# A one-core hybrid attention block in float32 pairs: SBUF tiles moved to other byte offsets, same instructions in the same order

## The chip, the core and the metric

The kernel runs on one core of one Trainium2 chip. The metric is the device time of one execution in microseconds; smaller is better. TensorE (PE) multiplies matrices: a load of weights (PEld) puts a block of 128 columns, the stationary operand, into the array, and a matmul then streams the moving operand past it and adds into PSUM. VectorE (DVE), ScalarE (ACT) and GpSimd (POOL) work on rows of 128 partitions. SyncE (SP) issues nearly all DMA transfers. The on-chip memory (SBUF) is 128 partitions wide; a tile has one byte offset that holds in all partitions, and this document is about these offsets.

## The reference, cut to what matters

The input x is 512 tokens by 2048 channels, float32. One decoder layer is computed:

```python
h = rmsnorm(x, norm_g)
proj = h @ w_in                     # 2048 -> 13 slices: qa, kca, vca, ksa, vsa, kwa, vwa, za, ga, qb, kb, vb, zb
# group A: 8 heads of 128, 2 kv heads; compressed, selected and windowed attention on rope'd q, k
kc = silu(blocks(rope(kca)) @ w1) @ w2 ; vc likewise     # blocks of 32 tokens, stride 16, 31 of them
o_a = g0 * attn(qa, kc, vc) + g1 * attn(qa, ksa, vsa; selected) + g2 * attn(qa, kwa, vwa; window)
y_a = o_a * silu(za)
# group B: 16 heads of 64, 2 kv heads, window of 128 tokens and a sink per head
y_b = attn(qb, kb, vb; window 128, sinks) * silu(zb)
x = x + concat(y_a, y_b) @ w_out
return rmsnorm(x, final_g)
```

With 512 tokens there are 8 blocks to select from and all are selected, so the selected attention is causal attention.

## The kernel before

**Numbers in pairs.** Nearly every float32 matrix is held as a pair: a rounded part (`F32R`, names with h or hi) and the rest (l or lo). One product of matrices is then three matmuls, written in `mm3` (lines 112 to 115): high by high, high by low, low by high. The first argument is the stationary operand, the other the moving one. The profile writes a matmul as `out<-moving,stationary`.

**Stages, in order of time.** (1) To about 55 us: `load_x` and `split_x` bring in x by its 16 slices of 128 channels, make the pair `xh`, `xl` and its sum of squares, and project the first slice of weights. (2) To 97 us: the second slice of `w0`, and the blocks tiles `F` (`blocks_part`) for the compressed keys and values. (3) To about 176 us: `tok_chunk` projects values with x as the stationary operand (moving operands of 256 and then 408 columns), interleaved with `compress_unit`, which multiplies `F` by streamed weights. (4) To about 440 us: eight heads of group A. `pair(h)` computes a head's q and gate by seven half-size products instead of eight (a Strassen-like scheme; `prod`, 128 by 256), with operand forms held in `xf`: the forms p and u lie in the `pu` tiles of the pool `yp`, the others in `xh`/`xl` and in spare halves of `KH`, `KL`, `VH`, `VL`. `attn_a` computes scores (`sp`, line 539), softmax on DVE and ACT, transposes (`tp<-ident,...`), and the products with the values (`op`). (5) To about 655 us: group B, eight pairs of heads, `proj` (128 by 512) and `softmax_b`, `attn_b`. (6) The rest: the output projection, first quarter 512 wide, the other three quarters with seven half-size products (`product`, 128 by 256), then the final norm.

Weights stream in through the pool `wp`: a raw tile (`raw`), from which ACT copies the rounded part `whi` and DVE subtracts to get `wlo` (`load_unit`, `unit`, `split_to`).

**What sets the order.** The order of instructions on each engine comes from the tile framework's planner together with `tc.issue_after`, by which the code ties a piece of work behind another.

**Where tiles lie.** A pool takes a stretch of SBUF from the left end upwards or, with `side="right"`, from the right end downwards, in the order in which pools are opened; inside it each tile is rounded up to 32 bytes. Left, from byte 1152: `const` (`ident` 512 bytes, `tab` 3588, `rstd` 16, `rstdb` 2048, `gates` 384, `gt` 64, `eps` 4), then `wp` and, before this change, `yp`, then the working pools (`s0`, later `wk`, later `so` and `wr`). Because `tab`, `rstd` and `eps` are not multiples of 64 bytes, `wp` begins at byte 7840, which is 61 times 128 and 32 more. All tiles above it have sizes that are multiples of 128 (but for a few small statistics), so **everything on the left that TensorE reads begins at 32 mod 128**: `whi`, `wlo`, the `F` and `pu` tiles, `qh`, `ql`, `ph`, `pl`. Only `ident` lies at 0. On the right the stack begins at byte 229344, which is 96 mod 128, so **`xh`, `xl`, `KH`, `KL`, `VH`, `VL`, and later `yh`, `yl` and the forms of the output projection begin at 96 mod 128**. Slices taken from these tiles start at multiples of 128 bytes from their beginning, except in the 408-column products, whose second half starts 1632 bytes in.

The built program holds 4808 matmuls with `F32R` operands: 2984 with a moving operand of 256 columns, 1536 of 512, 192 of 408 and 96 of 288. In 512 of them (464 left-with-left, which are the `pu` and `F` products, and 48 right-with-right) both operands begin at the same place mod 128; in 4200 they are 64 bytes apart; in the second halves of the 408-column products (96) they are 32 apart. The remaining matmuls are transposes and a few plain float32 ones.

Of the kernel before, what the change touches and what calls it, by code (L numbers as in the profile page):

```python
# [10 lines left out]
F32 = mybir.dt.float32  # L11
# [6 lines left out]
P = 128  # L18
S = 512
D = 2048  # L20
KT = D // P
NQ = S // P
# [5 lines left out]
CMP = 32  # L28
WARM = 40
FIRST = 1  # L30
TAB_W = 512 + NQ * CMP + 256 + 1


@with_exitstack
def hybrid_block(ctx, tc, xT, xtm, w0, w1s, w2s, wz, wq, wkb, wo0, wos, cw1, cw2, cpos, rope, tabs, sinks, gT, fg, out):
# [3 lines left out]
    def sb(name, bufs=1, side=None):  # L39
        return tc.tile_pool(name=name, bufs=bufs, side=side)  # L40

    const = ctx.enter_context(sb("const"))
    wp = ctx.enter_context(sb("wp", bufs=3))
    ident = const.tile([P, P], F32, name="ident")
    make_identity(nc, ident)
    tab = const.tile([P, TAB_W], F32, name="tab")
    dmask = tab[:, 0:512]
    cmask = tab[:, 512:512 + NQ * CMP]
    bmask = tab[:, 512 + NQ * CMP:768 + NQ * CMP]
    rowvalid = tab[:, TAB_W - 1:TAB_W]  # L50
    rstd = const.tile([P, NQ], F32, name="rstd")
    rstdb = const.tile([P, S], F32, name="rstdb")
    gates = const.tile([P, NQ, 24], F32, name="gates")
    gt = const.tile([P, KT], F32, name="gt")

    def dram(name, *shape):
        return tc.dram_tile(list(shape), F32, name=name)
# [5 lines left out]
    fd = dram("fd", 4, 2, P, KT // 4, 256)  # L63
    fw = dram("fw", 2, 2, P, KT // 4, 256)
    yd = [dram(f"yd{h}", P, S) for h in range(8)]
    eps = const.tile([P, 1], F32, name="eps")
    dve.memset(eps, EPS)
    act.activation(rstd[:, 0:1], eps, AF.Copy)

# [11 lines left out]
    def load_unit(src, width, rawp=None, opening=False):  # L81
# [9 lines left out]
                                       op=ALU.subtract).ins  # L91
        return hi, lo

    xstack = ctx.enter_context(ExitStack())
    xpool = xstack.enter_context(sb("xpool", side="right"))
    xh = xpool.tile([P, KT, S], F32R, name="xh")
# [23 lines left out]
        last["rope"] = dve.tensor_tensor(out=t2[64:128], in0=ps[0:64], in1=sin[0:64], op=ALU.mult).ins  # L120
        return t1, t2

    yp = ctx.enter_context(sb("yp"))
    p0 = ExitStack()
    s0 = p0.enter_context(sb("s0"))
    s0b = p0.enter_context(sb("s0b", bufs=2))
# [1120 lines left out]
def _tables():  # L1247
    def rope(d):
        inv = np.float32(10000.0) ** (-np.arange(0, d, 2, dtype=np.float32) / np.float32(d))
        ang = np.arange(S, dtype=np.float32)[None, :] * inv.astype(np.float32)[:, None]  # L1250
        return np.cos(ang.astype(np.float64)).astype(np.float32), np.sin(ang.astype(np.float64)).astype(np.float32)

    ca, sa = rope(128)
    cb, sb_ = rope(64)
    cb, sb_ = np.concatenate([cb, cb]), np.concatenate([sb_, sb_])
    ro = np.stack([np.concatenate([ca, ca]), np.concatenate([sa, -sa]),
                   np.concatenate([cb, cb]), np.concatenate([sb_, -sb_])], axis=1).astype(np.float32)
    p = np.arange(P)[:, None]
    j = np.arange(P)[None, :]
    caus = np.where(j <= p, 0.0, NEG)  # L1260
    band = np.where(j > p, 0.0, NEG)
    c = np.arange(CMP)[None, :]
    cm = [np.where((16 * c + 31 <= q * P + p) & (c < 31), 0.0, NEG) for q in range(NQ)]
    tabs = np.concatenate([np.zeros((P, 384)), caus] + cm + [band, caus, (p >= 31) * 1.0], axis=1).astype(np.float32)
    return np.ascontiguousarray(ro), np.ascontiguousarray(tabs)


# [51 lines left out]
```

## Time and profile before

| | |
|---|---|
| median of 3 runs | 831.02 us (827.9 to 832.21) |
| the profiled execution | 829.19 us; its span, first to last instruction, 827.4 us |
| granted TensorE clock in it | 0.997 |
| PE busy | 811.5 us, 98% of the span, 5278 matmul records |
| PE weight loads busy | 735.6 us (89%) |
| DVE / ACT / POOL busy | 662.1 (80%) / 485.6 (59%) / 89.3 us (11%) |
| DMA | 128.30 MB, 155 GB/s on average |

Matmuls are pipelined: the next starts before the last has ended, so the "mean ns of one" in the profile's groups is longer than the distance from one start to the next. The distance between starts, called the pace below, is what a product costs when TensorE is never idle. It is read from the timeline, whose first column is the start in us from the start of the span and whose second is the duration. A plain float32 matmul leaves two records.

### The profile page before, as it was taken

What the parts mean: (1) busy time and instruction counts of PE and PEld (TensorE: products, weight loads), DVE (VectorE), ACT (ScalarE), POOL (GpSimd) and SP (SyncE); (2) the same over time, 40 slices, a digit from 0 to 9 for tenths busy, and PEclk for the clock granted to TensorE, in tenths of its full rate; (3) what the DMA queues carried; (4) which work ended last, traced back from release to release, by engine and by line L of the source; (5) the groups of instructions that cost most, each with busy time, mean ns of one, the idle gap of its engine ahead of it and who ended that gap; (6) DMA issues with size and microseconds to landing.
All of it is one profiled execution on the core that took longest, in us unless ns stands there. A gap on an engine that the chain in (4) does not pass through costs nothing.

```text
span 827.4 us, 14161 instructions
## 1 busy us (share of the span) xinstructions
PE 811.5 (98%) x5278; PEld 735.6 (89%) x5278; DVE 662.1 (80%) x1311; ACT 485.6 (59%) x1026; POOL 89.3 (11%) x69
## 2 busy tenths in 40 slices
PE   9999999999999999999999999999999999999996
PEld 7788898999999999999888888888888788999996
DVE  6869786966799898999766688877677798877895
ACT  6734456564676786787665365645444647554555
POOL 3600002011001001101011121011011000110000
PEclk9999999999999999999999999999999999999998
DMA  9665885898330222522733321222222226797845
GB/s 324 194 206 166 281 290 200 265 371 284 103 111 22 99 77 92 166 90 89 251 107 102 99 92 56 74 80 74 77 76 77 77 62 241 235 251 198 244 96 203
DMA packets 52117, 128.30 MB, mean 155 GB/s; under 512 B 4945, under 2 KB 17233, under 8 KB 52049
## 3 DMA queue, kind: packets, MB, share of 16 engines
q1 hardware_dynamic: 50032, 120.59, 43.3%
q0 software_dynamic: 1728, 6.29, 4.3%
q8 instruction: 41, 0.67, 0.3%
q10 hardware_dynamic: 288, 0.52, 0.2%
q14 instruction: 28, 0.22, 0.1%
HBM read 110.31 MB, written 17.07 MB: 154 GB/s over the span
## 4 chain that ended last, share of the span: by engine, by line
PE 84%; DVE 6%; DMA 5%; issue 2%; ACT 2%; SPq 0%; DVEq 0%; ACTq 0%; POOLq 0%
PE pj L115 16%; PE pj L113 15%; PE pj L114 15%; PE bank L115 4%; PE bank L113 4%; PE oa L114 4%; PE oa L113 4%; PE oa L115 3%; PE sp L539 3%; PE bank L114 3%; PE tp L855 2%; DMA rw<-wos 1%; PE tp L577 1%; DMA xr<-xT 1%; DMA raw<-cw 1%
## 5 line engine op out<-in xcount | busy, mean ns | idle before, releaser
L115 PE MATMUL pj<-xh,wlo 128*128 128x512 f32 (+1 forms) x560 | 196.0, 350 | 2.0 <-DVE wlo L617 1.5
L113 PE MATMUL pj<-xh,whi 128*128 128x512 f32 (+1 forms) x560 | 196.2, 350 | 0.8 <-DVE t L665 0.8
L114 PE MATMUL pj<-xl,whi 128*128 128x512 f32 (+1 forms) x560 | 195.4, 349 | 0.0
L90 DVE TENSOR_TENSOR wlo<-raw,whi 128x1024 fp32r<-128x1024 f32 (+2 forms) x102 | 115.3, 1135 | 37.5 <-ACT whi L89 36.6
L89 ACT ACTIVATE whi<-raw 128x1024 fp32r<-128x1024 f32 (+1 forms) x101 | 95.2, 944 | 80.6 <-PE pj L114 24.0
L115 PEld LDWEIGHTS pj<-xh,wlo 128*128 128x128 f32 x560 | 105.3, 188 | 16.3 <-DVE wlo L617 2.2
L113 PEld LDWEIGHTS pj<-xh,whi 128*128 128x128 f32 x560 | 105.4, 188 | 14.2 <-DVE t L665 1.2
L114 PEld LDWEIGHTS pj<-xl,whi 128*128 128x128 f32 x560 | 105.3, 188 | 13.4 <-issue 0.7
L617 DVE TENSOR_TENSOR wlo<-raw,whi 128x1024 fp32r<-128x1024 f32 x49 | 61.6, 1260 | 10.3 <-ACT whi L616 9.9
L616 ACT ACTIVATE whi<-raw 128x1024 fp32r<-128x1024 f32 x49 | 51.7, 1056 | 24.7 <-PE pj L114 12.7
L113 PE MATMUL oa<-whi,yh 128*128 128x256 f32 (+1 forms) x168 | 50.1, 299 | 0.6 <-ACT yh L909 0.6
L114 PE MATMUL oa<-wlo,yh 128*128 128x256 f32 (+1 forms) x168 | 50.4, 300 | 0.2 <-DVE wlo L1147 0.2
L115 PE MATMUL oa<-whi,yl 128*128 128x256 f32 (+1 forms) x168 | 49.7, 299 | 0.0
L834 ACT ACTIVATE ttb<-ttb,mnb 128x256 f32<-128x256 f32 (+1 forms) x64 | 30.1, 471 | 26.0 <-DVE mnb L827 25.5
L509 DVE TENSOR_TENSOR pl<-tp,ph 128x512 fp32r<-128x512 f32 x56 | 37.6, 683 | 6.6 <-ACT ph L508 6.6
L508 ACT ACTIVATE ph<-tp 128x512 fp32r<-128x512 f32 x56 | 32.3, 592 | 17.9 <-PE tp L577 11.2
L114 PE MATMUL bank<-wlo,xh 128*128 128x256 f32 (+1 forms) x128 | 40.2, 316 | 0.0
L115 PE MATMUL bank<-whi,xl 128*128 128x256 f32 (+1 forms) x128 | 39.9, 314 | 0.0
L468 POOL TENSOR_TENSOR t<-t,t 128x512 f32<-128x512 f32 x9 | 19.3, 2147 | 176.4 <-DVE t L120 176.4
L113 PE MATMUL bank<-xh,whi 128*128 128x512 f32 x96 | 37.0, 396 | 1.1 <-ACT whi L89 0.7
L113 PE MATMUL bank<-whi,xh 128*128 128x256 f32 (+1 forms) x128 | 36.7, 318 | 1.3 <-ACT whi L89 1.3
L114 PE MATMUL bank<-xl,whi 128*128 128x512 f32 x96 | 37.0, 391 | 0.0
(356 smaller groups left out, 2202.2 us busy)
## 6 DMA issues: line engine op xcount, KB each, us to landing
raw<-wz SPq DMA_DIRECT2D x36, 512.0 KB, 3.6
raw<-wq SPq DMA_DIRECT2D x28, 512.0 KB, 3.7
raw<-cw SPq DMA_DIRECT2D x16, 512.0 KB, 5.0
raw<-wos SPq DMA_DIRECT2D x12, 512.0 KB, 5.0
rw<-wos SPq DMA_DIRECT2D x10, 512.0 KB, 5.5
xr<-xT SPq DMA_DIRECT2D x16, 256.0 KB, 5.0
raw<-w SPq DMA_DIRECT2D x8, 512.0 KB, 4.2
fd<-ft SPq DMA_DIRECT2D x4, 1024.0 KB, 5.9
```

The lines of the kernel that those rows point to most:

```text
L89: last["hi"] = act.activation(hi[:, :width], rw[:, :width], AF.Copy).ins
L90: last["lo"] = dve.tensor_tensor(out=lo[:, :width], in0=rw[:, :width], in1=hi[:, :width].bitcast(F32), op=ALU.subtract).ins
L113: pe.matmul(ps, ah, bh, start=first, stop=False, skip_group_check=go_on)
L114: pe.matmul(ps, ah, bl, start=False, stop=False, skip_group_check=go_on)
L115: recent["mm"] = pe.matmul(ps, al, bh, start=False, stop=last, skip_group_check=go_on).ins
L468: pool.tensor_tensor(out=t1, in0=t1, in1=t2, op=ALU.add)
L508: act.activation(ph, tp, AF.Copy)
L509: dve.tensor_tensor(out=pl, in0=tp, in1=ph.bitcast(F32), op=ALU.subtract)
L539: pe.matmul(sp[:, a:b], qq[:, qs], kk[0][:, ko:ko + b - a], start=pi == 0, stop=pi == 2)
L616: act.activation(hi, src, AF.Copy)
L617: last["lo"] = dve.tensor_tensor(out=lo, in0=src, in1=hi.bitcast(F32), op=ALU.subtract).ins
L834: act.activation(tv, tv, AF.Exp, bias=mn[:, e, v:v + 1], scale=-1.0, accum_out=dn[:, e, v:v + 1])
```

## The change

The sizes of a few small tiles and the place of one pool change. `tab` loses its last column (the row mask `rowvalid`), which moves to a seventeenth column of `gt`; `rstd` and `eps` become views of one 32-byte tile `small`. With this `wp`, and all that follows on the left, begins at a multiple of 128 bytes (7808). On the right a tile of 32 bytes, `edge`, is put at the very end, so everything else there begins at 64 mod 128. The pool `yp` (the `F`, `pu`, `yp` and `late` tiles, 32768 bytes) goes from the left side to the right side.

```diff
-TAB_W = 512 + NQ * CMP + 256 + 1
+TAB_W = 512 + NQ * CMP + 256
...
-    rowvalid = tab[:, TAB_W - 1:TAB_W]
-    rstd = const.tile([P, NQ], F32, name="rstd")
+    small = const.tile([P, 8], F32, name="small")
+    rstd, eps = small[:, 0:NQ], small[:, NQ:NQ + 1]
     rstdb = const.tile([P, S], F32, name="rstdb")
     gates = const.tile([P, NQ, 24], F32, name="gates")
-    gt = const.tile([P, KT], F32, name="gt")
+    gt = const.tile([P, KT + 1], F32, name="gt")
+    rowvalid = gt[:, KT:KT + 1]
...
-    eps = const.tile([P, 1], F32, name="eps")
...
+    edge = ctx.enter_context(sb("edge", side="right"))
+    edge.tile([P, 8], F32, name="edge")
+    yp = ctx.enter_context(sb("yp", side="right"))
     xstack = ctx.enter_context(ExitStack())
...
-    yp = ctx.enter_context(sb("yp"))
     p0 = ExitStack()
...
-    tabs = np.concatenate([np.zeros((P, 384)), caus] + cm + [band, caus, (p >= 31) * 1.0], axis=1).astype(np.float32)
+    tabs = np.concatenate([np.zeros((P, 384)), caus] + cm + [band, caus], axis=1).astype(np.float32)
...
-        "gT": a["norm_g"][0].reshape(KT, P).T,
+        "gT": np.concatenate([a["norm_g"][0].reshape(KT, P).T, (np.arange(P)[:, None] >= 31).astype(np.float32)], axis=1),
```

In the two built programs every engine has the same instructions in the same order with the same waits (8692 in each, 754 waits on PE, 1228 on DVE, 1047 on ACT, 539 on SP, 159 on POOL). What differs is addresses:

| operand | before, mod 128 | after, mod 128 |
|---|---|---|
| `whi`, `wlo`, `qh`, `ql`, `ph`, `pl` (left) | 32 | 0 |
| `F`, `pu`, `yp` tiles | 32 (left) | 64 (right) |
| `xh`, `xl`, `KH`, `KL`, `VH`, `VL`, `yh`, `yl`, forms of the output projection (right) | 96 | 64 |
| `ident`, `tab` | 0 | 0 |
| `rstdb`, `gates`, `gt` (not read by TensorE) | 64 | 32 |

Of the 4808 paired products, 4664 then have operands 64 bytes apart mod 128; 48 (the form p in one product of the last quarter, right with right) have them at the same place; the second halves of the 408-column products (96) stay 32 apart, their moving operand at 96. Apart from these 96, every operand of a paired product begins at a multiple of 64.

## The prediction
> **What bounds the kernel now.** I read the page's busy times first, then the chain that ended last, then the groups of PE with shapes kept apart, then the timeline, because only starts give the price of a product.
>
> ```profile
> PE 811.5 (98%) x5278; PEld 735.6 (89%) x5278; DVE 662.1 (80%) x1311; ACT 485.6 (59%) x1026; POOL 89.3 (11%) x69
> PEclk9999999999999999999999999999999999999998
> PE 84%; DVE 6%; DMA 5%; issue 2%; ACT 2%; SPq 0%; DVEq 0%; ACTq 0%; POOLq 0%
> ```
>
> TensorE is busy throughout at its full granted clock, and 84% of the chain is its own work. So the change can move the time only through the pace of products. It moves nothing but addresses: does the trace show a pace that depends on them? The groups first (out<-moving,stationary, count, mean ns of one):
>
> ```profile
> L113 PE MATMUL pj<-xh,whi 128*128 128x512 f32 x336 | 132.9, 396 | 0.4 <-DVE t L665 0.4
> L113 PE MATMUL pj<-xh,whi 128*128 128x256 f32 x224 | 63.3, 282 | 0.4 <-DVE t L665 0.4
> L113 PE MATMUL oa<-whi,yh 128*128 128x256 f32 x136 | 37.5, 276 | 0.0
> L113 PE MATMUL pj<-pu,whi 128*128 128x256 f32 x112 | 32.2, 287 | 0.0
> L228 PE MATMUL bank<-whi,F 128*128 128x256 f32 x64 | 16.7, 287 | 0.4 <-ACT whi L89 0.4
> L113 PE MATMUL bank<-whi,xh 128*128 128x256 f32 x64 | 16.9, 280 | 0.0
> L113 PE MATMUL oa<-ph,yh 128*128 128x256 f32 x16 | 4.5, 282 | 0.0
> ```
>
> Five groups of one shape, 256 columns, differ by 11 ns. The slow two, `pu` and `F` (287), have both operands at 32 mod 128. The fast one, `oa<-whi,yh` (276), has 32 and 96. `oa<-ph,yh`, in the same stage but with both at 96, takes 282. The starts give the paces (first and last row of unbroken stretches):
>
> ```profile
> 201.47 0.28 PE L113 MATMUL pj<-pu,whi 128*128 128x256 f32 x1
> 204.34 0.28 PE L113 MATMUL pj<-xh,whi 128*128 128x256 f32 x1
> ...
> 330.88 0.28 PE L113 MATMUL pj<-xh,whi 128*128 128x256 f32 x1
> 332.88 0.28 PE L115 MATMUL pj<-xh,wlo 128*128 128x256 f32 x1
> ...
> 711.61 0.28 PE L115 MATMUL oa<-whi,yl 128*128 128x256 f32 x1
> 731.79 0.28 PE L113 MATMUL oa<-whi,qh 128*128 128x256 f32 x1
> ...
> 599.68 0.40 PE L114 MATMUL pj<-xl,whi 128*128 128x512 f32 x1
> 601.31 0.40 PE L115 MATMUL pj<-xh,wlo 128*128 128x512 f32 x1
> ...
> 60.57 0.39 PE L113 MATMUL pj<-xh,whi 128*128 128x512 f32 x1
> 74.07 0.39 PE L113 MATMUL pj<-xh,whi 128*128 128x512 f32 x1
> ```
>
> - `pu`, equal places: 24 products in 2.87 us, 119.6 ns each.
> - `pj<-xh,whi`, 64 apart: 17 in 2.00 us, 117.6.
> - `oa`, 64 apart: 178 in 20.18 us, 113.4.
> - 512 columns: 7 in 1.63 us, 232.9; in the earlier stretch 59 in 13.50 us, 228.8.
>
> These paces share a step. 113.3, 120 and 233.3, each within 0.5 ns of a row above, are 17, 18 and 35 times 6.67 ns. 6.67 ns is also what 16 columns cost at the rate of the fastest stretch (113.3/17), and 16 float32 columns are 64 bytes. A moving operand of 256 columns that begins at 32 mod 64 lies on 17 blocks of 64 bytes; one that begins at 0 lies on 16. So I read 113.3 as "one step for each block touched, no collision", and 120 as that and one step lost against the weight load beside it. 512 columns touch 33 blocks (220 ns) and lose one to two steps more.
>
> A control is in the same trace. The 408-column products (1632 bytes) touch 26 blocks wherever a multiple of 32 begins, so by this reading the half with its moving operand at 0 mod 128 must not be faster than the half at 32:
>
> ```profile
> 153.77 0.35 PE L114 MATMUL bank<-wlo,xh 128*128 128x408 f32 x1
> 155.08 0.35 PE L115 MATMUL bank<-whi,xl 128*128 128x408 f32 x1
> ...
> 155.26 0.35 PE L113 MATMUL bank<-whi,xh 128*128 128x408 f32 x1
> 157.32 0.35 PE L115 MATMUL bank<-whi,xl 128*128 128x408 f32 x1
> ```
>
> At 32: 7 in 1.31 us, 187.1. At 0: 11 in 2.06 us, 187.3. Equal, and 28 steps. It fits, but "alignment does nothing" fits as well.
>
> **The change part by part.**
>
> *Left side to 0, right side to 64 mod 128.* Every moving operand of 256, 512 or 288 columns touches one block fewer: 16, 32, 18. The trace has no such product, so the saving s per product is bounded. Below: nothing (the 408 pair); it could be negative, since one placement shows two paces (117.6 and 113.3 with 64 apart), and that is a rival. Above: the bare number of blocks, 16 or 32 steps, 106.7 and 213.3 ns: from 228.8 to 232.9 that is 16 to 20 ns, from 117.6 it is 11, from 113.3 it is 6.7. I take one step, 6.67 ns: the nearest row is the step between 113.3 and 120, which is what one block more costs. Of 4808 paired products all but the 192 of 408 columns save it: 4616 x 6.67 ns = 30.8 us of TensorE time.
>
> *`yp` to the right.* 464 products (`pu` 336, `F` 128) go from equal places to 64 apart: 119.6 to 117.6 by the rows, 0.9 us more. That is within the rounding of the rest and I leave it out.
>
> *Small tiles.* `rowvalid` comes with `gt`, the first load, instead of with `tab`: 4 bytes per partition move from one transfer to another, no instruction and no wait changes; nothing, hidden by any transfer. `rstdb` goes from 64 to 32 mod 128 and DVE's other operands from 32 or 96 to 0 or 64. DVE rows of one shape:
>
> ```profile
> L458 DVE TENSOR_TENSOR zr<-pj,rstdb 128x512 f32<-128x512 f32 x9 | 6.2, 687 | 8.4 <-PE pj L115 8.4
> L910 DVE TENSOR_TENSOR yl<-yp,yh 128x512 fp32r<-128x512 f32 x16 | 10.4, 677 | 0.2 <-ACT yh L909 0.2
> ```
>
> One with an operand at 64, one with operands at 32 and 96: 10 ns of 680 apart, with a PSUM operand in the slower. I cost DVE, ACT and POOL at nothing.
>
> *How much of 30.8 us arrives.* By stage (span, PE, PEld, DVE, ACT, POOL busy with counts, PEclk, DMA share, GB/s):
>
> ```profile
> 0.00:55.00 55.00, 52.62 (x252) 42.55 (x253) 36.96 (x43) 34.88 (x55) 22.02 (x21) 1.00 0.78 264
> 97.00:128.00 31.00, 30.23 (x250) 29.41 (x249) 23.33 (x36) 17.22 (x27) 0.00 (x0) 1.00 0.89 308
> 198.00:300.00 102.00, 100.12 (x814) 97.65 (x813) 91.34 (x198) 73.52 (x179) 9.33 (x6) 1.00 0.28 92
> 440.00:655.00 215.00, 215.00 (x1120) 180.82 (x1119) 162.66 (x413) 109.54 (x263) 21.93 (x11) 1.00 0.25 78
> 700.00:780.00 80.00, 80.00 (x687) 79.09 (x686) 66.32 (x81) 40.92 (x59) 8.89 (x10) 1.00 0.83 234
> ```
>
> Sharing the 4616 out by the counts of such windows (warm-up, 408s and transposes taken off): 389 products to 97 us, 400 to 198, 1617 to 440, 1181 to 700, 1032 after. In steps: 2.6, 2.7, 10.8, 7.9, 6.9 us. What is late next eats a part of each:
>
> - To 198 us: the DMA share is 0.78 and 0.89, and in the chain the opening waits for loads (rows below); I keep 3.2 of 5.3.
> - Group A, 198 to 440: DVE is busy 91.34 of 102 us and would be 94% busy in the shorter stage; its chains (softmax, `wlo`) end later than a product that needs them more often. I keep 8.0 of 10.8.
> - Group B and the first quarter: DVE has a quarter of the time free; I keep 7.3 of 7.9.
> - The last three quarters: DMA share 0.83, and the chain ends through loads that do not get faster:
>
> ```profile
> 2.62 4.81 DMA xr<-xT
> 7.50 6.46 DMA xr<-xT
> 14.02 7.13 DMA raw<-w
> ...
> 775.22 7.02 DMA rw<-wos
> 792.48 5.23 DMA rw<-wos
> ```
>
> I keep 3.9 of 6.9. Sum: 22.4 us. The profiled execution took 829.19 us, so 806.8. The median of the runs, 831.02, is 1.8 above it: **808.6, taken as 808**. The shares kept are judgements; all 30.8 us would give 800, half of it 815.
>
> [...] The two paces of one shape, 119.6 and 113.3, differ only in where operands lie. [...]
>
> **The rivals.**
>
> *No change.* Products keep their paces because 32 mod 64 never cost anything, as the 408 pair allows; only the 464 equal ones gain, 0.9 us: 830. Against it: a least pace of exactly 17 steps for 16 blocks of data, which "nothing" does not explain.
>
> *Clean streams.* On whole blocks and 64 apart, matmul and weight load never meet: 512 columns fall to 32 steps, 256 to 16. From 230.5 (between the two rows) by 17.2 x 1536 = 26.4 us, from 117.6 by 10.9 x 1976 = 21.5, from 113.3 by 6.6 x 1008 = 6.7: 54.6 us, of which the shares above (22.4/30.8) let 40 through: 791. For it: 113.3 shows that a stretch without collision exists. Against: 512 columns lose one to two steps even at 64 apart, and the cause of that is not shown. [...]
>
> *Slower: another lock.* `bank<-whi,xh` (280) and `oa<-whi,yh` (276) have the same two places mod 128 and paces 4 ns apart, so the places alone do not decide; products settle into a rhythm with the weight loads. If the new places make the last stage's 1008 products settle at 120 instead of 113.3 (6.7 us) and the 1536 wide ones at 35 steps, 233.3, instead of 230.5 (4.3 us), the time is 831 + 11 = 842. It decides where the pace of 256 columns in the last stage comes out above 114 and that of 512 above 231.
>
> **How the numbers follow.** One step, with half to all of it arriving (800 to 815, and somewhat beyond): 0.55. Clean (784 to 800): 0.21. No change: 0.13. Slower: 0.11. Differences of 0.5%, 4 us, are what a measurement can tell from none. Faster 0.55 + 0.21 + 0.01 for a small gain, 0.77; same 0.12; slower 0.11. The range 790 to 831 leaves out the slower case (0.11), a third of no change (0.04) and the lowest quarter of clean (0.05), 0.2 in all.
>
> **What would show it.** Right: `pu` and `F` groups from 287 to 276 or less, `oa<-whi,yh` from 276 to about 270, 512 columns from 396 to about 389, the 408s unchanged; waits of PE on DVE in group A longer; DVE's own durations unchanged. Wrong if 512 columns stay at 396 or if PE's pace falls and the stages keep their length.

## The result and the profile after

| | before | after |
|---|---|---|
| median of 20 runs each | 831.68 us (827.9 to 833.68) | 828.78 us (826.9 to 831.9) |
| ratio, 95% interval | | 0.9975 [0.9963, 0.9987] |
| the profiled execution | 829.19 us, span 827.4 | 826.90 us, span 825.1 |
| PE busy | 811.5 us | 810.0 us |

The forecast was 808 us. The kernel did not change by as much as the 0.5% that the prediction called a difference. In a second series of 12 runs the same changed kernel stood at 1.0006 [0.9988, 1.0023] of the kernel before, so even the small gain of the first series did not repeat. The outcome is nearest to the rival *No change* (830). A ratio is an estimate from all runs of both kernels, not the quotient of the two medians.

The page of after, busy times, granted clock and the chain that ended last:

```profile
PE 810.0 (98%) x5278; PEld 734.5 (89%) x5278; DVE 664.1 (80%) x1311; ACT 485.2 (59%) x1026; POOL 89.7 (11%) x69
...
PEclk9999999999999999999999999999999999999999
...
PE 82%; DVE 6%; DMA 5%; ACT 3%; issue 2%; POOL 1%; SPq 0%; DVEq 0%; ACTq 0%; POOLq 0%
```

The groups of PE in after, shapes kept apart (out<-moving,stationary, count, mean ns of one), in the order in which they were shown of before:

```profile
L116 PE MATMUL pj<-xh,whi 128*128 128x512 f32 x336 | 132.7, 395 | 0.4 <-DVE t L667 0.4
L116 PE MATMUL pj<-xh,whi 128*128 128x256 f32 x224 | 63.2, 282 | 0.4 <-DVE t L667 0.4
L116 PE MATMUL oa<-whi,yh 128*128 128x256 f32 x136 | 37.5, 276 | 0.0
...
L116 PE MATMUL pj<-pu,whi 128*128 128x256 f32 x112 | 31.9, 285 | 0.0
...
L230 PE MATMUL bank<-whi,F 128*128 128x256 f32 x64 | 16.3, 283 | 0.0
...
L116 PE MATMUL bank<-whi,xh 128*128 128x256 f32 x64 | 16.7, 276 | 0.0
...
L116 PE MATMUL oa<-ph,yh 128*128 128x256 f32 x16 | 4.5, 282 | 0.0
```

512 columns (396 to 395), `xh` (282), `oa<-whi,yh` (276) and `oa<-ph,yh` (282) stand where they stood. Only `pu` (287 to 285), `F` (287 to 283) and the value projection `bank<-whi,xh` (280 to 276) moved. The timeline gives paces, start to start (first and last row of unbroken stretches of after):

```profile
199.38 0.28 PE L116 MATMUL pj<-pu,whi 128*128 128x256 f32 x1
202.21 0.28 PE L116 MATMUL pj<-xh,whi 128*128 128x256 f32 x1
...
203.43 0.28 PE L117 MATMUL pj<-xl,whi 128*128 128x256 f32 x1
208.49 0.28 PE L118 MATMUL pj<-xh,wlo 128*128 128x256 f32 x1
...
702.17 0.28 PE L116 MATMUL oa<-whi,ph 128*128 128x256 f32 x1
719.98 0.28 PE L117 MATMUL oa<-wlo,uh 128*128 128x256 f32 x1
...
568.47 0.40 PE L118 MATMUL pj<-xh,wlo 128*128 128x512 f32 x1
580.37 0.40 PE L118 MATMUL pj<-xh,wlo 128*128 128x512 f32 x1
...
597.04 0.39 PE L118 MATMUL pj<-xh,wlo 128*128 128x512 f32 x1
602.77 0.39 PE L116 MATMUL pj<-xh,whi 128*128 128x512 f32 x1
```

`pu`: 24 in 2.83 us, 117.9 ns (119.6 before). `xh`: 43 in 5.06, 117.7. `oa`: 157 in 17.81, 113.4, as before, though its rows now begin on whole blocks of 64 bytes. 512 columns: 51 in 11.90, 233.3, and later in the same stage 25 in 5.73, 229.2: two paces of one stream in one execution, as before (232.9 and 228.8).

Summed over all groups of at least 16 products (mean pace after less mean pace before, times the count), the paces explain 2.1 us of gain; the profiled execution gained 2.3. So what gain there was went through TensorE's pace, as the prediction held, and the pace did not do what it said. The parts: `pu` and `F` 1.0 us, their neighbour `bank<-whi,xh` and its two companions 0.65 us (116.9 to 113.5, 192 products), the 408s and the 512s with a few tenths each.

### The profile page after: what moved, and what is told of

Read it like the earlier page. It is cut to its first block, busy times and chain, and to the rows that moved or that the text cites. A ratio compares the mean times of both kernels' runs of the same rounds, so it can differ in the third digit from the quotient of the medians.

```text
span 825.1 us, 14161 instructions
## 1 busy us (share of the span) xinstructions
PE 810.0 (98%) x5278; PEld 734.5 (89%) x5278; DVE 664.1 (80%) x1311; ACT 485.2 (59%) x1026; POOL 89.7 (11%) x69
## 4 chain that ended last, share of the span: by engine, by line
PE 82%; DVE 6%; DMA 5%; ACT 3%; issue 2%; POOL 1%; SPq 0%; DVEq 0%; ACTq 0%; POOLq 0%
PE pj L118 15%; PE pj L117 15%; PE pj L116 15%; PE bank L118 4%; PE oa L117 4%; PE bank L116 4%; PE oa L116 4%; PE oa L118 3%; PE bank L117 3%; PE sp L541 3%; DMA rw<-wos 2%; PE tp L857 2%; PE tp L579 1%; DMA xr<-xT 1%; DMA raw<-cw 1%
```

## The experiments

Each expectation uses the names of theories that stood at its time; the text around it says what they were.

**One part alone: `yp` to the right, nothing else.** Everything keeps its place at an odd multiple of 32; only `pu` and `F` come 64 bytes from their partners.

```diff
+    yp = ctx.enter_context(sb("yp", side="right"))
     xstack = ctx.enter_context(ExitStack())
...
-    yp = ctx.enter_context(sb("yp"))
```

> Only the pool yp goes to the right side; nothing is shifted, left tiles stay at 32 mod 128, right tiles at 96, so every operand is still an odd multiple of 32 and the pu and F products get operands 64 bytes apart. Theory A (only equal places mod 128 have a price, whole blocks of 64 bytes none): all of the change's gain, 2 us, ratio 0.9975; pu groups at 283 to 285 ns, F at 279 to 283. Theory B (the recorded one: one 64-byte block less per product is worth something): less than the change's gain, at most the 0.9 us of the 464 products, ratio 0.999 or above.

830.82 us against 830.12, ratio 0.9993 [0.9976, 1.001]. Judged by its time, theory A missed (it expected the whole gain) and B's number came out; the paces say the opposite. `pu` fell from 119.2 to 117.6 ns, `F` from 119 to 115 and the value projection from 117 to 113.5, the same as in after, with no operand on a whole block. What kept the time up was the last stage, which nothing had touched: it went from 113.4 to 117.7 ns, and its group from a mean of 276 to 281:

```profile
L114 PE MATMUL oa<-whi,yh 128*128 128x256 f32 x136 | 38.2, 281 | 0.0
```

**The other part alone: the shift by 32 bytes, `yp` left where it was** (the lines are against after).

```diff
-    yp = ctx.enter_context(sb("yp", side="right"))
     xstack = ctx.enter_context(ExitStack())
...
+    yp = ctx.enter_context(sb("yp"))
```

> The other part alone: all tiles at multiples of 64 (left 0, right 64 mod 128), but yp stays on the left, so the pu and F products keep operands at the same place mod 128. Theory A: nothing, ratio 1.000 with 831.7 us, pu groups at 285 to 287 and F at 283 to 287 as before. Theory B: some of the gain is here, ratio below 0.999.

828.55 us, 0.999 [0.997, 1.0009], a time that does not decide between the theories. The paces do: all are as before, `pu` and `F` at 119 ns, the last stage at 113.4, though every moving operand of 256, 512 or 288 columns now lies on one block fewer. The shift itself does nothing to the pace.

```profile
L115 PE MATMUL oa<-whi,yh 128*128 128x256 f32 x136 | 37.6, 276 | 0.0
L115 PE MATMUL pj<-pu,whi 128*128 128x256 f32 x112 | 32.2, 287 | 0.0
```

**All operands at the same place mod 128.** After, with the edge tile 64 bytes larger; `zr` and, in the same way, `kb1` are halved to make room.

```diff
-    edge.tile([P, 8], F32, name="edge")
+    edge.tile([P, 24], F32, name="edge")
...
-        zr = wk.tile([P, 2, S], F32, name="zr", tag="xr", bufs=1)[:, 0, :]
+        zr = wk.tile([P, S], F32, name="zr", tag="xr", bufs=1)
```

> The right side moved on by 64 bytes, so that 4488 of 4808 paired products have both operands at 0 mod 128 (a tile that only half was used of, zr and kb1, is halved to make room). Theory A: each pays what equal places cost in the trace of before: 256 columns at 119 to 120 ns instead of 113.4 (about 1200 products in the value projection and the last stage, 6 to 7 us) or 117.7 (1700 products, 3 us); 512 columns between nothing and one step of 6.67 ns (0 to 10 us): 840 to 850 us, ratio 1.012 to 1.025. Rival C (a place costs nothing, paces belong to stages): ratio 1.000.

831.79 us, 1.0015 [1.0001, 1.003], far from the 840 to 850 of theory A. 256 columns rose to 119 to 120, as the theory of a price for equal places said, but 512 columns got *faster*, and so the time rose by little. Later the same kernel was timed again:

> The kernel with equal places again, timed. Theory D (equal places leave one rhythm per shape): one heap of times within 0.15%, 831.4 to 832.7 as before, and 512 columns again at 226.7 to 228.4, 256 at 119 to 120. Rival (the paces there were one draw of a rhythm): two heaps, and 512s at 230 or above in this profile.

832.8 us, 1.004 [1.0024, 1.0055]. The timeline of that second execution in group A and in group B:

```profile
203.63 0.28 PE L117 MATMUL pj<-xl,whi 128*128 128x256 f32 x1
208.79 0.28 PE L118 MATMUL pj<-xh,wlo 128*128 128x256 f32 x1
...
569.06 0.40 PE L118 MATMUL pj<-xh,wlo 128*128 128x512 f32 x1
580.65 0.39 PE L118 MATMUL pj<-xh,wlo 128*128 128x512 f32 x1
```

43 products in 5.16 us, 120.0 ns (117.7 in after); 51 in 11.59, 227.3 ns (233.3). The mean of all 512s is near 228, of the 256s of the last stage 120.0, the same in both executions. Its 12 times ran from 831.7 to 835.17: none as low as the others reach, but over 0.4% and not within the 0.15% expected.

**A bench of bare products.** The block is left out and the output is zeros: 32 equal products of each kind (48 in the rows with the kernel's pattern of three), the moving operand at a growing distance.

> Not the block: a bench of matmuls with paired operands (moving 256 or 512 columns, a new weight load for each) at chosen places, 32 or 48 in a row, each row with a PSUM tile of its own name; the output is zeros. Names: n256s32d64x is 256 columns, stationary at 32 mod 128, moving 64 further on; r: moving operand in the low area, stationary in the high one; k: both in one area; t and v: the kernel's pattern of three (high high, high low, low high) with moving high or low. Theory A: a step of about 6 ns at distance 0 mod 128 and nothing else; no difference between stationary at 0 and at 32; 113.4 ns for 256 columns at distance 64. Theory B: places at whole blocks (s0 with d0 or d64) faster by 6.67 ns than s32. The stages' two paces at 64 apart (113.4 and 117.7) are open: either the roles (r and v against s and t) or the pattern of three make them.

The stationary operand at 0 or at 32 mod 128 made no difference above 0.4 ns but for one row (256 columns at the label 32: 117.2 against 118.75 ns). 256 columns: 117.2 to 119.4 ns, and 113.75 at the distance labelled 64. 512 columns: 231.9 to 234.4, and 227.2 at 112. With the roles exchanged, the moving operand in the low area, the rows of three took 120.0, 119.0 and 117.7 ns at the labels 0, 32 and 64, against 118.5, 117.3 and 113.5. Only later did I notice that the two areas of this bench lie 128 bytes further apart mod 256 than its labels say: 64 is 192 and 112 is 240.

**The same kernels again, one execution each.** By now one theory (D) said that a stream of products has several rhythms and that what went before picks one; the other (E) that the addresses fix it.

> The kernel before once more, unchanged, to look at its paces in another execution. The times of before lie in two heaps, about 828.7 and about 832.2 us, and the profiled execution, 829.19, is of the lower one. Theory D (products settle into one of two rhythms, and which one a stage gets differs between executions of one program): the last stage's 256-column products at 113.4 ns as before where this execution takes under 830 us, at 117.7 (groups oa at 280 to 281 instead of 276) where it takes over 831. Theory E (the rhythm is fixed by the addresses): 113.4 whatever the time.

> The kernel with only yp moved, unchanged from the first experiment, whose profiled execution (830.93 us) had the last stage at 117.7 ns. Theory D: 117.7 again if the execution takes about 831 us, 113.4 if it takes under 829. Theory E: 117.7 in any case, since the addresses are the same.

> The changed kernel once more. Theory D: last stage at 113.4 if the execution takes about 828, at 117.7 if above 830. Theory E: 113.4 in any case. In both: pu and F products as in the first profile, pu about 117.7, value projection 113.5.

Before: 831.35 us, last stage at 113.4 as in its first profile; theory D had expected 117.7 for so long a time, and missed. Its paces sum to within 0.4 us of those of the first execution, and yet it took 2.2 us longer. `yp` to the right: 831.71, last stage again at 117.7, the value projection now 116.7 instead of 113.5. After: 830.59, and its last stage, 113.4 in the first profile, now between 116 and 118, as the group's mean shows beside 276:

```profile
L116 PE MATMUL oa<-whi,yh 128*128 128x256 f32 x136 | 38.1, 280 | 0.0
```

One program, the same addresses, two paces: here D was right, and E, that the addresses alone fix the pace, fell. The 20 times of after fall into 14 below 829.2 and 6 from 829.9 up. About 1000 products of the last stage at 4 ns are 4 us; that this is the whole of the two heaps is not shown, since before took 831.35 with its last stage at 113.4.

**Repeated streams in one execution** (again a bench with zeros as output). A and B are 256 columns at a distance of 192 bytes with roles exchanged, Z is 256 columns at 128, V 512 columns at 128, W 512 columns at 192, E 512 columns at 240 (mod 256).

> The bench again, now one stream repeated in one execution: A is 256 columns, moving high at 64, stationary low at 0 (113.75 ns in the first bench); B the roles changed (117.8); Z both at 0 (118.4); W, V, E 512 columns at distance 64, 0, 112 (233.1, 232.5, 227.2). They follow one another in changing order, then after one product of 260 to 320 columns (a kick of the phase), then after TensorE stood still. Theory D: a stream's pace changes with what went before it, A is seen at 117 to 118 and B at 113 to 114 somewhere. Theory E: each stream has the pace of the first bench every time.

The timeline of that bench, 32 products a row:

```profile
38.66 3.93 PE L44 MATMUL s0Ax<-hi,lo 128*128 128x256 f32 x32
42.43 3.93 PE L44 MATMUL s1Bx<-lo,hi 128*128 128x256 f32 x32
46.20 3.81 PE L44 MATMUL s2Ax<-hi,lo 128*128 128x256 f32 x32
49.85 3.96 PE L44 MATMUL s3Zx<-hi,lo 128*128 128x256 f32 x32
53.65 3.81 PE L44 MATMUL s4Ax<-hi,lo 128*128 128x256 f32 x32
57.30 3.96 PE L44 MATMUL s5Zx<-hi,lo 128*128 128x256 f32 x32
61.10 3.80 PE L44 MATMUL s6Bx<-lo,hi 128*128 128x256 f32 x32
64.75 7.62 PE L44 MATMUL s7Wx<-hi,lo 128*128 128x512 f32 x32
...
94.50 7.71 PE L44 MATMUL s12Ex<-hi,lo 128*128 128x512 f32 x32
102.05 7.61 PE L44 MATMUL s13Vx<-hi,lo 128*128 128x512 f32 x32
```

Distances of starts over 32: A 117.8, then 114.1 and 114.1; B 117.8, then 114.1; Z 118.8 both times. With one product of 264, 280, 288 or 304 columns ahead A was fast (113.8 to 114.4 ns), with one of 260, 268, 272 or 320 slow (117.5 to 118.1); in the four rows shortly after TensorE had stood still for 0.69 us it took 117.8, 113.8, 117.8 and 113.8. So D held for this distance; what picks the rhythm is not shown, since the stream before the odd product changed too. The stream E, 512 columns at 240 mod 256, took 235.9 and later 236.6 ns, where the first bench had 227.2 at the same addresses: the widest gap between two rhythms in these runs.

**512s equal, 256s apart.** The runs with all places equal suggested a version better than both kernels: weight tiles with 128 bytes more, used from byte 64 on where 512-column products read them (against after; the calls that pass `wide` are left out).

```diff
+    def pieces(at=0):
+        return [wp.tile([P, 1056], F32R, name=nm, tag=nm)[:, at:at + 1024] for nm in ("whi", "wlo")]
...
-        hi = wp.tile([P, 1024], F32R, name="whi", tag="whi")
-        lo = wp.tile([P, 1024], F32R, name="wlo", tag="wlo")
+        hi, lo = pieces(16 if wide else 0)
```

> After, but the weight tiles are 4224 bytes instead of 4096 and the stages with 512-column products use them from byte 64 on: 1488 of the 1536 products of 512 columns then have both operands at the same place mod 128, all others stay as after (2936 of 256 columns 64 apart). The tile of zr and of kb1 is halved to make room. Theory D (a product settles into one of several rhythms, and equal places leave only one): the 512s keep the 226.7 to 228.4 ns of the kernel with all places equal, the 256s keep their two rhythms (113.4 and 117.8); 1488 x about 2.7 ns (230.3 to 227.6) = 4.0 us, most of it arriving: 824 to 826. Theory B2 (the 227 there was a rhythm of that one program, since the bench showed 232.5 for 512 columns at equal places): 512s at 230 to 233, time 828 to 832.

> The changed kernel again, timed on the same chip as the mixed one. Theory D: two heaps of times, near 828 and near 830.3, and one of the two rhythms per stage in the profile. Rival: one heap at 828.8.

831.28 us, 1.0023 [1.001, 1.0036]: my own expectation missed. After, beside it, 831.08 us: 11 of 12 runs at 830.55 or more and one at 826.97, not the two heaps that theory D expected, and its profiled execution had the last stage at 116 to 118 ns again. The miss of the mixed kernel was the key. A tile of 4224 bytes is 16.5 times 256, so neighbouring weight tiles alternate between 0 and 128 **mod 256**. Sorted by that distance the 512s of this profile split: a mean of 228.3 ns from start to start where a product and the next lie at 0 (542 of them), 232.6 to 233.1 where either lies at 128 (843). Two stretches of its group B, the first at 0, the second at 128:

```profile
575.82 0.39 PE L118 MATMUL pj<-xh,whi 128*128 128x512 f32 x1
581.03 0.39 PE L120 MATMUL pj<-xh,wlo 128*128 128x512 f32 x1
...
603.47 0.40 PE L118 MATMUL pj<-xh,whi 128*128 128x512 f32 x1
608.83 0.39 PE L120 MATMUL pj<-xh,wlo 128*128 128x512 f32 x1
```

23 products in 5.21 us, 226.5 ns, and 23 in 5.36, 233.0. Sorted in the same way the 512s of every profile so far fell in order (in after a mean of 230.1 ns for `pj<-xh,whi` and its two companions, at 64, and 233.3 for those with `yh`, at 192), and the 256s (119.2 for `pu` of before, at 0; 117.8 for `pu` of after, at 64; 113.4 or 117.7 for the last stage, at 192) but for a few small groups (`opb<-ph,VB` of group B, at 192, takes 118 to 119 ns); mod 128 had not done that: the 226.5 and the 233.0 above lie at the same distance mod 128. By this theory (F) the kernel before and after have the same distances for all but 464 products, because both sides moved down by 32 bytes.

**Distances set mod 256.** Weight tiles of 4352 bytes, 17 times 256. The first kernel puts 1488 products of 512 columns at 0 mod 256. The second changes nothing mod 128: it moves only the weights of group A by 128 bytes, which brings 1092 products of 256 columns from 64 to 192 mod 256 (and 84 the other way). The third does both; the edit to `unit` below is in the second and third, and the second does without the shift for the 512s. Four small tiles share space in pairs, which adds one DVE instruction. The first pair of lines of the diff is against the mixed kernel.

```diff
-        return [wp.tile([P, 1056], F32R, name=nm, tag=nm)[:, at:at + 1024] for nm in ("whi", "wlo")]
+        return [wp.tile([P, 1088], F32R, name=nm, tag=nm)[:, at:at + 1024] for nm in ("whi", "wlo")]
...
     def unit(raw):
-        hi, lo = pieces()
+        hi, lo = pieces(32)
```

> After, but the weight tiles are 4352 bytes (17 times 256) and the stages with 512-column products use them from byte 64 on, so that 1488 products of 512 columns have both operands at the same place mod 256; the 256-column products stay 64 or 192 apart mod 256 as after. Four small tiles share their space in pairs and zr is halved to make room, which adds one DVE instruction. Theory F (the pace follows the distance of the operands mod 256, not mod 128): 512s at 227.5 to 228.5 (from 230.3 at 64 and 233.2 at 192), 1296 x 2.3 ns + 192 x 5.3 ns = 4.0 us, so 825 to 827 against 829 to 831. Rival (equal places mod 128 decide): 512s as in the mixed kernel, 229.4 to 231.6, time 829 to 832.

> After with the 4352-byte weight tiles of the run above, but only the weights of the eight heads of group A begin 128 bytes further: 1008 of their products of 256 columns then lie 192 instead of 64 apart mod 256 (64 apart mod 128 in both). Theory F: these go from 117.7 to the 113.4 to 117.5 of the last stage, which lies at 192 mod 256: 0 to 4.3 us less. Theory D alone (history decides): no change of the group's pace, 117.7, and 829 to 831. By the distance mod 128 nothing changes at all.

> Both edits: 512s at the same place mod 256 and group A's 256s at 192 mod 256. Theory F: the sum of the two runs above, 822 to 827. Rival: as after, 829 to 831.

| | median | ratio to before | mean 512s, group B | mean `pj<-xh,whi` 256 | last stage |
|---|---|---|---|---|---|
| 512s at 0 (12 runs) | 826.06 us | 0.9955 [0.9936, 0.9973] | 228.0 ns | 117.8 ns | 113.4 ns |
| group A at 192 (12 runs) | 828.63 us | 0.9971 [0.9955, 0.9987] | 230.2 | 115.6 | 117.8 |
| both (6 runs) | 825.12 us | 0.9947 [0.9928, 0.9965] | 228.0 | 115.9 | 113.3 |

The times of the first and the third came out as theory F said. The time of the second fits F as well, but it is no proof: the kernel it was made from, after, stood at 0.9975 in its first series and at 1.0006 in its second. Its paces are the proof. The timeline of the first in the same stretch of group B, then two stretches of the second in group A:

```profile
566.82 0.40 PE L120 MATMUL pj<-xh,wlo 128*128 128x512 f32 x1
578.39 0.39 PE L120 MATMUL pj<-xh,wlo 128*128 128x512 f32 x1
```

```profile
295.37 0.28 PE L118 MATMUL pj<-xh,whi 128*128 128x256 f32 x1
299.61 0.28 PE L118 MATMUL pj<-xh,whi 128*128 128x256 f32 x1
...
356.32 0.28 PE L118 MATMUL pj<-xh,whi 128*128 128x256 f32 x1
359.16 0.28 PE L119 MATMUL pj<-xl,whi 128*128 128x256 f32 x1
```

First: 51 products in 11.57 us, 226.9 ns, where after took 233.3. Second: 36 products in 4.24 us, 117.8 ns, and 25 in 2.84, 113.6. So the mean of 115.6 is a mixture of the two rhythms; at the distance of 64, in after, all twelve unbroken stretches of 20 products or more of this group in group A ran at 117.7 to 118.1 ns. The paces of the first sum to 5.2 us less than before, and its profiled execution (823.95 us, the fastest of its twelve) is 5.2 us shorter than that of before; the medians, 826.06 against 830.42, are 4.4 us apart. In the third the sum is 7.8 us and 5.5 arrived (823.66 us). In the second the sum is 0.3 us, because its last stage fell into the slow rhythm, and its profiled execution, 831.37 us, was 2.2 us longer than that of before. The 2 us by which the second and the third fall short of their sums were not followed up; that is about as much as the 2.2 us between the two executions of before at the same paces.

**The sweep.** A bench with zeros as output, in the kernel's pattern of three, 36 products a row; the number behind `d` is the distance of the moving from the stationary operand mod 512.

> A bench that leaves the block out (output zeros): the pattern of three of the kernel, 36 products each, moving operand 0 to 480 bytes past the stationary one mod 512 in steps of 32, for 512 and 256 columns; then roles exchanged at 0, 64, 128, 192. Theory F: 512 columns 227 to 228.5 at 0 and 256, about 230 at 64 and 320, 232 at 128 and 384, 233 at 192 and 448, a period of 256; 256 columns 119 to 120 at 0, 117.5 at 64, 118.8 at 128, 113.4 to 117.5 at 192. Rival (mod 128): 0, 128, 256, 384 alike, 64 and 192 alike.

The timeline, 512 columns and then 256:

```profile
37.87 8.33 PE L46 MATMUL n512d0x<-hi,lo 128*128 128x512 f32 x36
46.04 8.57 PE L46 MATMUL n512d32x<-hi,lo 128*128 128x512 f32 x36
54.44 8.41 PE L46 MATMUL n512d64x<-hi,lo 128*128 128x512 f32 x36
62.69 8.57 PE L46 MATMUL n512d96x<-hi,lo 128*128 128x512 f32 x36
...
104.73 8.35 PE L46 MATMUL n512d256x<-hi,lo 128*128 128x512 f32 x36
112.91 8.57 PE L46 MATMUL n512d288x<-hi,lo 128*128 128x512 f32 x36
...
171.60 4.48 PE L46 MATMUL n256d0x<-hi,lo 128*128 128x256 f32 x36
175.92 4.41 PE L46 MATMUL n256d32x<-hi,lo 128*128 128x256 f32 x36
...
197.21 4.28 PE L46 MATMUL n256d192x<-hi,lo 128*128 128x256 f32 x36
201.32 4.42 PE L46 MATMUL n256d224x<-hi,lo 128*128 128x256 f32 x36
...
231.18 4.28 PE L46 MATMUL n256d448x<-hi,lo 128*128 128x256 f32 x36
235.29 4.42 PE L46 MATMUL n256d480x<-hi,lo 128*128 128x256 f32 x36
```

| distance mod 256 | 0 | 32 | 64 | 96 | 128 | 160 | 192 | 224 |
|---|---|---|---|---|---|---|---|---|
| 512 columns, ns | 226.9 | 233.3 | 229.2 | 233.6 | 233.3 | 234.2 | 233.3 | 233.3 |
| again, 256 further | 227.2 | 233.3 | 229.4 | 233.6 | 233.3 | 234.2 | 233.3 | 233.1 |
| 256 columns, ns | 120.0 | 117.8 | 118.1 | 119.4 | 118.9 | 117.2 | 114.2 | 118.3 |
| again, 256 further | 119.4 | 118.1 | 117.8 | 119.7 | 118.6 | 117.5 | 114.2 | 118.1 |

Within these rows the paces repeat after 256 bytes, to within 0.6 ns, and not after 128: 0 and 128 differ by 6 ns for 512 columns, 64 and 192 by 4 ns for both widths. With roles exchanged, 0, 64, 128 and 192 gave 227.5, 229.4, 232.2, 233.6 and 119.7, 117.8, 118.6, 113.9. Two limits: the second half of the sweep runs in the order of the first, so a rhythm set by the row before would repeat as well, and in steps of 32 bytes the 240 with its two paces, 227.2 and 236, is not seen. The stationary operand stands at 0 mod 256 in the whole sweep; that the distance counts, and not the place of the moving operand, is shown by the kernels: moving both by 32 bytes changed no pace (the last stage 113.4 ns, `pu` and `F` 119, as before), moving the weights alone by 64 or 128 bytes did (a stretch of 512s of group B from 233.3 to 226.9 ns, the 256s of group A from 117.8 to 113.6 in a part of their stretches). What in the chip has this period no run shows.

## Why the prediction was wrong, step by step

The measured 828.78 us lies inside the stated range of 790 to 831, but only in the part of it that was there for the rival *No change*; nothing of the mechanism that gave 808 was seen, and the 512s stayed where they were (395 ns, forecast 389), which the prediction had named as the sign of being wrong.

*What bounds the kernel: right.* The time went with the sum of PE's paces (2.1 us of 2.3 after, 5.2 of 5.2 with the 512s moved). That single executions agree so closely is partly luck: the two of before differ by 2.2 us at the same paces.

*"Every moving operand touches one block fewer ... I take one step, 6.67 ns": wrong, and this step alone made the forecast.* The two rows it rested on were right, 113.4 and 119.6 ns for 256 columns, but the difference is the distance of the two operands mod 256, 192 against 0, and not where the stream begins. The change moved the left side from 32 to 0 and the right side from 96 to 64: both down by 32, so the distance of nearly every product stayed what it was. Before and after have 1296 of the 512s at 64 and 240 at 192; of the 256s, 336 (`pu`) went from 0 to 64 and 128 (`F`) from 0 to 192, and the rest stayed. Two readings led there. Six groups of 256 columns were shown, not five, and the steps between their paces were taken for counts of blocks; but 113.4 ns stayed 113.4 when the streams lay on 16 blocks instead of 17, and 117.8 and 229.2 are no whole number of steps. And "6.67 ns is also what 16 columns cost at the rate of the fastest stretch" was no second witness: 256 columns in 113.4 ns are 7.09 ns for 16, and 6.67 comes out only when the 17 blocks are put in. Against whole blocks spoke the control in the same trace, the 408s, equal at 0 and at 32; the prediction saw it and gave the reading that alignment does nothing a chance of 0.13.

*"I leave it out", the 0.9 us of `yp`: the term that was there.* `pu` and `F` gained 1.0 us, and the value projection, which runs between the products of `F`, 0.65 us more, that I had not counted. That the two are linked is likely but not shown: the same value projection stood at 113.5 and at 116.7 ns in two executions of the kernel with only `yp` moved.

*Small tiles at nothing: right.* The DVE rows of the prediction take 686 and 680 ns after (687 and 677).

*"How much of 30.8 us arrives": not tested by the change.* No run tells what share would have arrived of a gain of 30.8 us. With the 512s at 0 mod 256, 4.4 of 5.2 us arrived by the medians, more than the 22.4 of 30.8 that the prediction kept, but the interval of that gain, 2.2 to 5.3 us, holds its share too. (Its five counts of products add to 4619 instead of 4616, which changes nothing.)

*The rival "No change": right in the main.* The equal products gained what it said (1.0 us against 0.9); the value projection and some tenths of the 408s and 512s came on top. The objection to it, that nothing explains a least pace of 17 steps, falls with the sweep, where that pace (114.2 ns there) belongs to the distance 192.

*The rival "another lock": the rhythms are real, but the new places did not bring them.* The same program ran its last stage at 113.4 and at 116 to 118 ns, above the 114 that the rival named as the point from which it decides; in that execution the sum of paces rose by about 3 us over the first one of after. The slow one came as well with `yp` moved alone, where the last stage kept its addresses. It was 117.8 ns and not 120, and the 512s did not join in, so the kernel did not come out slower than before. The wording "the places alone do not decide" holds at 192 bytes, where one program showed both.

*The rival "Clean streams": not seen.* The fastest stretches shown here ran at 113.4 ns for 256 columns and 226.5 for 512, not at the 106.7 and 213.3 of bare blocks. The pace went with the distance of the two operands instead: in the sweep a product of 256 columns took 114.2 ns with 192 bytes between them and 120.0 with both at the same place.

## What to carry to other kernels

Before a layout is changed, list for every group of products the quantity that a theory says matters, before and after: here one column, the distance of the two operands mod 256, would have shown that 4344 of 4808 products don't change at all. When two numbers fit a ratio of small integers, look for the row that would break it, and give that row its weight. For float32 products fed this way, keep 512-column operands at the same place mod 256 (226.9 ns in the sweep, 229.2 to 234.2 at the other distances) and 256-column ones 192 bytes apart (114.2 ns, 117.2 to 120.0 at the others), and judge a few per mille by many runs, since after ran its last stage in two rhythms (113.4 and 116 to 118 ns), and before took 829.19 and 831.35 us at the same paces.

## What the runs showed of the hardware that I had not expected

- The pace of a product with its weight load depends on the distance of the two SBUF addresses and repeats after 256 bytes: in the sweep 226.9 to 234.2 ns for 512 columns, 113.9 to 120.0 for 256. The best distance for 512 columns, 0 (226.9 and 227.2 ns), is with 96 the slowest for 256 (120.0 and 119.4 at 0, 119.4 and 119.7 at 96).
- The place of the operands against 32 or 64 bytes does not show in the pace (both moved by 32 bytes: all paces of the kernel the same, the last stage at 113.4 ns, `pu` and `F` at 119). Which of the two is the moving one shows little in the sweep (113.9 against 114.2 ns at 192; 1.1 ns at the most, for 512 columns at 128); in the first bench the exchanged rows of three were 1.5 to 4.2 ns slower, at 192 by as much as its two rhythms differ.
- At some distances a stream has two rhythms: 114.1 or 117.8 ns at 192 for 256 columns, 229.2 or 233.3 at 64 and 227.2 or 236 at 240 for 512. At 192 it changed with an odd product or a pause of 0.69 us ahead; for 512 columns at 64 and 240 that was not tried. At distance 0 the means of groups stayed within 226.7 to 228.5 (512 columns) and 119.0 to 120.0 (256) where nearly all products of a width lay there.
- Addresses alone, but for one DVE instruction more, took 0.53% [0.35, 0.72] off the kernel before (both edits, 6 runs); the 512s at distance 0 alone took 0.45% [0.27, 0.64], so what the second edit adds is not told apart from nothing.
